# A decoder trunk on one core: the 72 weight pieces kept in DRAM are loaded, split and stored in three calls

## The chip, the cores and the metric

The kernel runs on one core of a Trainium2 chip. The metric is the device time of one execution in microseconds. Engines are named as the profile names them: PE (TensorE matmuls; PEld its weight loads), DVE (VectorE), ACT (ScalarE), POOL (GpSimd), and SP, whose queue issues every DMA of this kernel in order (SPq in the trace).

## The reference, cut to what matters

One sequence of 256 tokens, model width 1024, passes through two layers. Each has a half-step SwiGLU FFN (hidden width 2816) before and after its mixer; the mixer of layer 0 is a gated short convolution, that of layer 1 is RWKV-7 time mixing.

```python
def swiglu(x, w_gu, w_d):
    gate, up = jnp.split(x @ w_gu, 2, axis=-1)
    return (jax.nn.silu(gate) * up) @ w_d

for i in range(DEPTH):                       # DEPTH = 2
    x = x + 0.5 * swiglu(rms_norm(x, norm_g[i, 0]), ffn_w_gu[i, 0], ffn_w_d[i, 0])
    h = rms_norm(x, norm_g[i, 1])
    x = x + (short_conv_mixer(h, ...) if i % 2 == 0 else rwkv7_mixer(h, ...))
    x = x + 0.5 * swiglu(rms_norm(x, norm_g[i, 2]), ffn_w_gu[i, 1], ffn_w_d[i, 1])
return rms_norm(x, final_g)
```

Everything is float32. The kernel gets float32 accuracy from PE by splitting each operand in a rounded part `hi` and a rest `lo`, and adding three products: hi by hi, hi by lo, lo by hi.

## The kernel before, in words

The order of work is FFN 0, the convolution, FFN 1, FFN 2, the RWKV mixer, FFN 3. An FFN has 11 chunks (`c`) of 256 hidden columns, gate and up; each chunk takes two weight tiles (`kh` 0 and 1) of 1 MB. Then `project_out` (L246) takes the down projection in six groups, `[1, 2, 2, 2, 2, 2]` tiles of 1 MB. The convolution has six chunks and three groups, `[1, 1, 2]`.

Each weight tile goes through `weights` (L88): SP loads `raw`, ACT casts it into `hi` (L104), DVE subtracts to give `lo` (L105). There are three buffers each of `raw`, `hi` and `lo`, so SP runs at most three weight tiles ahead of DVE, and DVE at most three ahead of PE.

Between these loads the kernel prepares 72 pieces of weights for later: 48 of the RWKV matrices, 16 of its output matrix, 8 of FFN 3. A piece is 128 by 512 floats. `part_some(n)` (L602) first stores to DRAM whatever the call before has split (the tiles `hl`, hi and lo side by side, 512 KB), then takes n new pieces: it loads each into a tile `raw` (256 KB), casts it on ACT (L615) and subtracts on DVE (L616). It is called with n = 2 at the start of every chunk of FFN 0, the convolution, FFN 1 and FFN 2 until the pieces run out, which is in chunk 7 of FFN 2. `narrow` (L622) reads a piece back when the RWKV mixer wants it.

Two tags of buffers matter. `hl` has 7 buffers, for pieces on their way out, pieces read back, and two tiles `wboth`. `raw` has 2 buffers, for `raw_p` and for the two tiles `wa1` of `mixed_lora` (L628). `mixed_lora` is called between the convolution and FFN 1; it loads two small matrices into `wa1`, and POOL computes the two `wboth` from them (L642, L644), which stay until the mixer.

All loads and stores go through `load` (L48), which pins the DMA behind everything that was written before it for SP. So SP's order is the program's order, and a DMA whose wait isn't over holds up all that follow. ACT and DVE also work in the order of their instruction streams; that order is set when the program is built, by a planner that puts an instruction where its inputs are expected to be ready, except where it is pinned. The first weight tile of a layer (`kh` 0 of chunk 0) is loaded in the last group of the layer before; its `kh` 1 is loaded in chunk 0, and the norm's remaining steps (`late`) are run between its matmuls.

Of the kernel before, what the change touches and what calls it, by code (L numbers as in the profile page):

```python
# [21 lines left out]
FT = F // 128  # L22
# [3 lines left out]
class Trunk:  # L26


    def __init__(self, ctx, tc, bufs):
        self.tc, self.nc = tc, tc.nc  # L30
        nc = tc.nc
        self.const = ctx.enter_context(tc.tile_pool(name="const", bufs=1))
        self.rwp = ctx.enter_context(tc.tile_pool(name="rwp", bufs=1))
        self.front = ctx.enter_context(tc.tile_pool(name="front", bufs=1))
        self.dram = ctx.enter_context(tc.tile_pool(name="dram", bufs=1, space=bass.MemoryType.DRAM))
        self.parts, self.to_part, self.to_store = {}, deque(), deque()
        self.trp = ctx.enter_context(tc.tile_pool(name="trp", bufs=2, space=bass.MemoryType.PSUM))
        self.turn = False
        self.raw_bufs, self.hi_bufs, self.lo_bufs = bufs
        self.fixed = self.const.tile([128, 1298], F32, name="fixed")  # L40
        self.fixed_used = 0
        self.ident = self.fixed_cols(128)
        make_identity(nc, self.ident)
        self.x = self.const.tile([128, 2, D], F32, name="x")
        self.nhalf = self.fixed_cols(8)
        nc.gpsimd.memset(self.nhalf, -0.5)
# [164 lines left out]
    def norm_rows(self):  # L211


        nc = self.nc
        now, xn = {}, {}
        after = SimpleNamespace(first=None, late=deque())
        after.ready = [self.narrow(("k", 0, i), "k") for i in range(3)]

        def turn(t):

            out = []
            for h in range(2):
                out.append(self.tr_bank("hT"))
                for j in range(4):
                    nc.tensor.transpose(out=out[h][:, j * 128:(j + 1) * 128],
                                        in_=xn[t][:, h * 512 + j * 128:h * 512 + (j + 1) * 128], identity=self.ident)
            return out

        def step(t, h, c0=0, n=512):
            if h == 0:  # L230
                now["sq"] = self.halves(t)
            half, rstd = now["sq"]
            half(h)
            if h == 1:
                rs = rstd()
                xn[t] = self.wide([128, D], "xn")
                for i in range(2):
                    hs = slice(i * 512, i * 512 + 512)
                    nc.vector.tensor_scalar(xn[t][:, hs], self.x[:, t, hs], rs, None, op0=ALU.mult)
            if t == 1 and h == 0:  # L240
                after.banks = turn(0)

        after.turn = turn
        return step, after

    def project_out(self, ah, al, kt, w_out, alpha, groups, step, out, kc=2):  # L246

        nc = self.nc
        acc = [[self.mm_bank(f"acc{t}{h}") for h in range(2)] for t in range(2)]
        k0, posts = 0, deque()  # L250
        keep = lambda z: z
        for n in groups:
            ws = [self.weights(w_out[(k0 + kc * i) * 128:(k0 + kc * i + kc) * 128, :].rearrange("(k p) n -> p k n", p=128),
                               [128, kc, D], "o") for i in range(n)]
            last = k0 + kc * n == kt
            if last:
                keep = self.tc.keep_in_program_order
                if out is not None and out.first:
                    out.ready.append(out.first())
            for t in range(2):  # L260
                for h in range(2):

                    fine = out is None and t == h == 1
                    ts, size = slice(t * 128, t * 128 + 128), 256 if fine and last else 512
                    for c in range(0, 512, size):
                        hs = slice(h * 512 + c, h * 512 + c + size)
                        ps = (self.mm_bank(f"acc{c}") if fine and last else acc[t][h])[:, 0:size]
                        for k in range(k0, k0 + kc * n):
                            (wh, wl), j = ws[(k - k0) // kc], (k - k0) % kc
                            self.product(ps, ah[:, k, ts], al[:, k, ts], wh[:, j, hs], wl[:, j, hs],  # L270
                                         k == (k0 if fine and last else 0),
                                         k == kt - 1 or fine and k == kt - kc * groups[-1] - 1, keep)
                        if last or fine and k0 + kc * n == kt - kc * groups[-1]:
                            xs = self.x[:, t, hs]
                            nc.vector.scalar_tensor_tensor(xs, ps, alpha, xs, ALU.mult, ALU.add)
                        if last:
                            posts.append(step(t, h, c, size))
                    if last:
                        for _ in range(t + (t > h)):
                            post = posts.popleft()  # L280
                            if post:
                                post()
            k0 += kc * n
        if out is not None and posts[-1]:
            out.late.extend((lambda: None, posts.pop()))
# [35 lines left out]
                        normed.late.popleft()()  # L321
        return ps

    def ffn(self, normed, w_gu, w_d, follow, beside=True):
        nc, tc = self.nc, self.tc
        with tc.tile_pool(name="ffn", bufs=1, side="right", reuse_waits="tile") as pool, \
                (nullcontext() if normed.ps else self.banks(mm=6)):
# [3 lines left out]
            if normed.ps:  # L331
                normed.ready.extend(self.ffn_weights(w_gu, 1, kh) for kh in range(2))
            for c in range(FT // 2):
                if beside:
                    self.part_some(2)
                ps = (normed.ps if normed.ps and c == 0 else
                      self.inner(normed, "gu", lambda c, kh: self.ffn_weights(w_gu, c, kh), c))
                pt = self.tr_bank("aT").rearrange("p (j t) -> p j t", j=2)
# [9 lines left out]
                                            identity=self.ident)  # L348
                self.split(ah[:, 2 * c:2 * c + 2], al[:, 2 * c:2 * c + 2], pt)
            step, out = follow()  # L350
            self.project_out(ah, al, FT, w_d, 0.5, [1, 2, 2, 2, 2, 2], step, out)
        return out

    def conv(self, normed, w_in, cw, w_out, follow):

        nc, tc = self.nc, self.tc
        with tc.tile_pool(name="conv", bufs=1, reuse_waits="tile") as pool, self.banks(mm=6):
# [3 lines left out]
            cT = pool.tile([128, KT, T], F32, name="cT")  # L361
            project = lambda c: self.inner(normed, "ci", lambda c, kh: self.conv_weights(w_in, c, kh), c)
            for c in range(4):
                self.part_some(2)
                ps = project(c)
                pt = self.tr_bank("zT").rearrange("p (j t) -> p j t", j=2)
                for t in range(2):
# [12 lines left out]
                    nc.vector.scalar_tensor_tensor(cT[:, k, 2:], pt[:, j, :T - 2], cw[:, 0, k:k + 1], cT[:, k, 2:],  # L380
                                                   ALU.mult, ALU.add)
            for c in range(2):
                self.part_some(2)
                ps = project(4 + c)
                b = pool.tile([128, 2, 512], F32, name="b", tag="b", bufs=2)
                for t in range(2):
# [215 lines left out]
    def part_some(self, n):  # L602

        nc = self.nc
        while self.to_store:
            key, hl = self.to_store.popleft()
            self.parts[key] = self.dram.tile([128, 2, 512], F32, name="parts_%d" % len(self.parts))
            self.load(self.parts[key], hl)
        for _ in range(min(n, len(self.to_part))):
            key, src = self.to_part.popleft()  # L610
            raw = self.rwp.tile([128, 512], F32, tag="raw", name="raw_p", bufs=2)
            self.load(raw.rearrange("p (k n) -> p k n", k=2) if len(src.shape) == 3 else raw, src)
            hl = self.part_tile("hl_p")
            hi = hl[:, 0].bitcast(F32R)
            nc.scalar.copy(hi, raw)  # L615
            nc.vector.tensor_tensor(hl[:, 1].bitcast(F32R), raw, hi.bitcast(F32), ALU.subtract)  # L616
            self.to_store.append((key, hl))

    def part_tile(self, name):
        return self.rwp.tile([128, 2, 512], F32, tag="hl", name=name, bufs=7)  # L620

    def narrow(self, key, name):  # L622

# [4 lines left out]
    def mixed_lora(self, mu, w1, a1):  # L628
# [1 line left out]
        nc = self.nc  # L630
        out = []
        for k0 in range(0, KT, 4):
            w = self.rwp.tile([128, 4, 128], F32, tag="raw", name="wa1", bufs=2)
            for i, src in enumerate((w1, a1)):
                self.load(w[:, :, 64 * i:64 * i + 64],
                          src[k0 * 128:k0 * 128 + 512].rearrange("(k p) n -> p k n", p=128))
# [197 lines left out]
    def rwkv_heads(self, pool, prm, krv, lora, gT, g2, rows, row_tile, P, loaded, follow,  # L834
# [201 lines left out]
        def feed():  # L1036

            if done[0] >= len(P):
                for j, z in enumerate(first_weights):
                    sources.insert(2 * j, (None, *z))  # L1040
            while sources and (done[1] < 7 or sources[0][2]):
                i, key, to = sources.popleft()
                if to:
                    for j in range(2):
                        self.load(to[j], self.parts[key][:, j].rearrange("p (k n) -> p k n", k=2))
                else:
                    loaded.setdefault(i, []).append(self.narrow(key, "n"))
                    done[1] += 1
# [77 lines left out]
def trunk_kernel(ctx: ExitStack, tc: tile.TileContext, x, norm_g, final_g, ffn_w_gu, ffn_w_d, conv_w_in, conv_w,  # L1126
# [29 lines left out]
    with k.wide_weights():  # L1156
# [3 lines left out]
        posts = [step(t, h) for t, h in ((1, 0), (0, 1), (1, 1))]  # L1160
        n.late.extend((lambda: [post() for post in posts[0:2]], posts[2]))
        cv = []
        n = k.ffn(n, ffn_w_gu[0, 0], ffn_w_d[0, 0], lambda: before(
            lambda: cv.append(k.channel_vectors(72, [mu[0], conv_w[0]]).rearrange("p (m k) -> p m k", k=KT)),
            lambda: k.norm_T(g[:, 1], lambda: k.conv_weights(conv_w_in[0]))))
        cv, = cv
        n = k.conv(n, conv_w_in[0], cv[:, 6:9], conv_w_out[0], lambda: before(k.wkv_constants, lambda: k.norm_T(g[:, 2], fw(0, 1))))
        wa1 = k.mixed_lora(cv, w1[0], a1[0])
        n = k.ffn(n, ffn_w_gu[0, 1], ffn_w_d[0, 1], lambda: k.norm_T(g[:, 3], fw(1, 0)))
        n = k.ffn(n, ffn_w_gu[1, 0], ffn_w_d[1, 0], lambda: before(lambda: k.part_some(0), k.norm_rows))  # L1170
    n = k.rwkv(n, g[:, 4], cv[:, 0:6], wa1, dict(
        w_rkv=w_rkv[0], w0=w0, w2=w2[0], a0=a0, a2=a2[0], g1=g1[0], g2=g2[0],
        k_k=k_k[0], k_a=k_a[0], r_k=r_k[0].rearrange("h j -> (h j)"), ln_w=ln_w[0], ln_b=ln_b[0], w_o=w_o[0]),
# [26 lines left out]
```

## Time and profile before

| what | value |
|---|---|
| median of 3 runs | 1141.81 us (1140.89 to 1142.64) |
| the profiled execution, its own time | 1145.31 us |
| its span in the trace | 1143.6 us |
| mean granted clock of TensorE | 0.982 of full speed |
| PE busy | 1095.9 us, 96% of the span |
| DVE, ACT, POOL busy | 710.0, 562.0, 107.0 us |
| moved by DMA | 256.19 MB, mean 224 GB/s |

The profile comes from one execution, 3.5 us longer than the median. Busy time is the time in which an engine had an instruction running, for PE also when it ran at half clock. The granted clock has two levels, 1.0 (2.4 GHz) and 0.5 (1.2 GHz); a value between is a mean over a stretch.

### The profile page before, as it was taken

To read this page: it belongs to the slowest core of one execution; us is meant where nothing else is said; L and a number is where in the kernel's file an instruction comes from. 1 tells how busy PE (TensorE), PEld (TensorE's weight loads), DVE (VectorE), ACT (ScalarE), POOL (GpSimd) and SP (SyncE) were. 2 spreads that over 40 slices of the span, in tenths; PEclk is the share of its full clock that TensorE was granted. 3 is DMA by queue.
4 is the path that set the end of the run, shared out by engine and by line. 5 is a ranking of instruction groups with operands and counts; after the bars stand their busy time and mean duration, and the time that the engine had idled before them with its cause. 6 is when DMAs were issued, how large, how long until landed. Compare 5 with 4: busy or idle time off the path is not lost.

```text
span 1143.6 us, 15921 instructions
## 1 busy us (share of the span) xinstructions
PE 1095.9 (96%) x6064; PEld 906.1 (79%) x6064; DVE 710.0 (62%) x1021; ACT 562.0 (49%) x893; POOL 107.0 (9%) x201
## 2 busy tenths in 40 slices
PE   6999999899959999998999999999999999999997
PEld 4788888688848888886888888998887767888886
DVE  4666544677546665446665534757999986555535
ACT  6555433555435554345554433356666536444423
POOL 5000000000200000000000001022343221000000
PEclk9999999899979999998999999999999999999999
DMA  8999756697299995549997651963442656656541
GB/s 295 360 331 335 243 182 205 221 328 259 76 313 323 348 340 202 189 161 326 353 329 240 222 184 32 315 221 126 131 141 64 194 176 201 203 184 204 184 184 37
DMA packets 164340, 256.19 MB, mean 224 GB/s; under 512 B 10414, under 2 KB 128934, under 8 KB 164264
## 3 DMA queue, kind: packets, MB, share of 16 engines
q1 hardware_dynamic: 164264, 255.17, 66.5%
q8 instruction: 48, 0.79, 0.3%
q14 instruction: 28, 0.23, 0.1%
HBM read 216.34 MB, written 38.80 MB: 223 GB/s over the span
## 4 chain that ended last, share of the span: by engine, by line
PE 57%; issue 26%; DVE 10%; ACT 3%; DMA 2%; POOL 1%; SPq 0%; POOLq 0%; ACTq 0%; DVEq 0%
PE gu L111 10%; PE gu L112 10%; PE gu L110 10%; PE acc L112 5%; PE acc L110 5%; PE acc L111 5%; PE pj L110 2%; DVE pd L518 1%; PE aT L347 1%; PE pj L111 1%; PE pj L112 1%; PE xr L54 1%; DMA raw_p<-in_rwkv_w_rkv_dram 1%; PE ch L54 1%; PE G L54 1%
## 5 line engine op out<-in xcount | busy, mean ns | idle before, releaser
L110 PE MATMUL gu<-hi_gu,xh 128*128 128x512 f32 x688 | 271.8, 400 | 14.5 <-ACT hi_gu L104 13.8
L111 PE MATMUL gu<-lo_gu,xh 128*128 128x512 f32 x688 | 276.9, 403 | 5.0 <-DVE lo_gu L105 5.0
L105 DVE TENSOR_TENSOR lo_gu<-raw_gu,hi_gu 128x2048 fp32r<-128x2048 f32 (+2 forms) x92 | 197.9, 2154 | 130.9 <-ACT hi_gu L104 130.8
L112 PE MATMUL gu<-hi_gu,xl 128*128 128x512 f32 x688 | 274.9, 400 | 0.0
L104 ACT CAST hi_gu<-raw_gu 128x2048 fp32r<-128x2048 f32 (+2 forms) x92 | 165.0, 1797 | 72.8 <-PE gu L112 43.9
L105 DVE TENSOR_TENSOR lo_o<-raw_o,hi_o 128x2048 fp32r<-128x2048 f32 x48 | 109.3, 2291 | 116.5 <-ACT hi_o L104 116.5
L110 PEld LDWEIGHTS gu<-hi_gu,xh 128*128 128x128 f32 x688 | 131.4, 191 | 42.6 <-ACT hi_gu L104 15.2
L111 PEld LDWEIGHTS gu<-lo_gu,xh 128*128 128x128 f32 x688 | 132.2, 192 | 34.3 <-DVE lo_gu L105 8.2
L112 PEld LDWEIGHTS gu<-hi_gu,xl 128*128 128x128 f32 x688 | 132.1, 192 | 26.3 <-DVE xl L178 0.4
L104 ACT CAST hi_o<-raw_o 128x2048 fp32r<-128x2048 f32 x48 | 90.9, 1909 | 105.9 <-PE acc L112 102.3
L112 PE MATMUL acc<-hi_o,al 128*128 128x512 f32 (+1 forms) x356 | 138.1, 388 | 0.0
L111 PE MATMUL acc<-lo_o,ah 128*128 128x512 f32 (+1 forms) x356 | 138.0, 388 | 0.0
L110 PE MATMUL acc<-hi_o,ah 128*128 128x512 f32 (+1 forms) x356 | 132.2, 388 | 0.0
L148 POOL TENSOR_TENSOR rs<-ms,fixed 128x1 f32<-128x1 f32 x14 | 8.8, 632 | 862.4 <-DVE ms L146 862.3
L341 ACT ACTIVATE s<-gu,rs 128x256 f32<-128x256 f32 x88 | 41.7, 475 | 91.9 <-PE gu L112 91.3
L111 PEld LDWEIGHTS acc<-lo_o,ah 128*128 128x128 f32 x356 | 66.9, 188 | 13.5
L112 PEld LDWEIGHTS acc<-hi_o,al 128*128 128x128 f32 x356 | 66.9, 188 | 13.4
L110 PEld LDWEIGHTS acc<-hi_o,ah 128*128 128x128 f32 x356 | 66.9, 188 | 13.2
L115 ACT CAST ah<-aT 128x512 fp32r<-128x512 f32 x44 | 25.7, 583 | 87.6 <-PE aT L347 87.6
L345 DVE SCALAR_TENSOR_TENSOR a<-gu,rs,s 128x256 f32<-128x256 f32 x88 | 41.8, 480 | 28.5 <-ACT s L341 28.4
L616 DVE TENSOR_TENSOR hl_p<-raw_p,hl_p 128x512 fp32r<-128x512 f32 x72 | 47.3, 687 | 15.9 <-ACT hl_p L615 15.6
L116 DVE TENSOR_TENSOR al<-aT,ah 128x512 fp32r<-128x512 f32 x44 | 30.3, 689 | 40.7 <-ACT ah L115 40.7
(263 smaller groups left out, 1629.7 us busy)
## 6 DMA issues: line engine op xcount, KB each, us to landing
raw_gu<-in_ffn_w_gu_dram SPq DMA_DIRECT2D x164, 512.0 KB, 7.0
raw_o<-in_ffn_w_d_dram SPq DMA_DIRECT2D x44, 1024.0 KB, 5.0
parts<-hl_p SPq DMA_DIRECT2D x72, 512.0 KB, 4.8
hl_n<-parts SPq DMA_DIRECT2D x52, 512.0 KB, 4.0
raw_p<-in_rwkv_w_rkv_dram SPq DMA_DIRECT2D x48, 256.0 KB, 5.4
raw_ci<-in_conv_w_in_dram SPq DMA_DIRECT2D x14, 512.0 KB, 8.1
raw_ci<-in_conv_w_in_dram SPq DMA_DIRECT2D x4, 1024.0 KB, 8.2
raw_o<-in_conv_w_out_dram SPq DMA_DIRECT2D x4, 1024.0 KB, 4.8
```

What stands on the lines that cost most here:

```text
L54: self.tc.keep_in_program_order(self.nc.tensor.matmul(out, lhsT, rhs, start=True, stop=True))
L104: nc.scalar.copy(hi[:, ks], raw[:, ks])
L105: nc.vector.tensor_tensor(lo[:, ks], raw[:, ks], hi[:, ks].bitcast(F32), ALU.subtract)
L110: keep(mm(out, xh, wh, start=start, stop=False))
L111: keep(mm(out, xh, wl, start=False, stop=False))
L112: keep(mm(out, xl, wh, start=False, stop=stop))
L115: keep(self.nc.scalar.copy(hi, src))
L116: keep(self.nc.vector.tensor_tensor(lo, src, hi.bitcast(F32), ALU.subtract))
L341: act = nc.scalar.activation(s, ps[t][:, 0:256], AF.Silu, scale=rstd[t])
L345: nc.vector.scalar_tensor_tensor(a, ps[t][:, 256:512], rstd[t], s, ALU.mult, ALU.mult)
L347: nc.tensor.transpose(out=pt[:, j, t * 128:t * 128 + 128], in_=a[:, j * 128:(j + 1) * 128], identity=self.ident)
L616: nc.vector.tensor_tensor(hl[:, 1].bitcast(F32R), raw, hi.bitcast(F32), ALU.subtract)
```

## The change

`part_some` gets three stages in three successive calls: a call stores what the call before it split, splits what the call before it loaded, and loads n new pieces. The piece is loaded straight into the second half of its `hl` tile and split in place, so the `raw` tag goes away; `hl` gets 8 buffers, and `wa1` takes two of them. Calls are spread: 1 and 2 in turn in the chunks of an FFN (from chunk 2 on in FFN 0), and 1 at the start of each group of `project_out`, except in FFN 3. `norm_rows`, which runs between the chunks and the groups of FFN 2, calls `part_some(2)` until nothing is left to load or split. In the mixer's heads, `feed` may hold 8 read-back pieces in place of 7.

```diff
@@ norm_rows
+        while self.to_part or self.to_split:
+            self.part_some(2)
         now, xn = {}, {}
         after = SimpleNamespace(first=None, late=deque())
         after.ready = [self.narrow(("k", 0, i), "k") for i in range(3)]
@@ project_out(..., step, out, beside=True, kc=2)
         for n in groups:
+            if beside:
+                self.part_some(1)
             ws = [self.weights(...) for i in range(n)]
@@ ffn(self, normed, w_gu, w_d, follow, beside=True, first=0)
             for c in range(FT // 2):
-                if beside:
-                    self.part_some(2)
+                if beside and c >= first:
+                    self.part_some(1 + c % 2)
...
-            self.project_out(ah, al, FT, w_d, 0.5, [1, 2, 2, 2, 2, 2], step, out)
+            self.project_out(ah, al, FT, w_d, 0.5, [1, 2, 2, 2, 2, 2], step, out, beside)
@@ conv
             for c in range(4):
-                self.part_some(2)
+                self.part_some(1 + c % 2)
...
             for c in range(2):
-                self.part_some(2)
+                self.part_some(1)
@@ part_some
             key, hl = self.to_store.popleft()
             self.parts[key] = self.dram.tile([128, 2, 512], F32, name="parts_%d" % len(self.parts))
             self.load(self.parts[key], hl)
+        while self.to_split:
+            key, hl = self.to_split.popleft()
+            hi, lo = hl[:, 0].bitcast(F32R), hl[:, 1]
+            nc.scalar.copy(hi, lo)
+            nc.vector.tensor_tensor(lo.bitcast(F32R), lo, hi.bitcast(F32), ALU.subtract)
+            self.to_store.append((key, hl))
         for _ in range(min(n, len(self.to_part))):
             key, src = self.to_part.popleft()
-            raw = self.rwp.tile([128, 512], F32, tag="raw", name="raw_p", bufs=2)
+            hl = self.part_tile("hl_p")
+            raw = hl[:, 1]
             self.load(raw.rearrange("p (k n) -> p k n", k=2) if len(src.shape) == 3 else raw, src)
-            hl = self.part_tile("hl_p")
-            hi = hl[:, 0].bitcast(F32R)
-            nc.scalar.copy(hi, raw)
-            nc.vector.tensor_tensor(hl[:, 1].bitcast(F32R), raw, hi.bitcast(F32), ALU.subtract)
-            self.to_store.append((key, hl))
+            self.to_split.append((key, hl))
@@ part_tile
-        return self.rwp.tile([128, 2, 512], F32, tag="hl", name=name, bufs=7)
+        return self.rwp.tile([128, 2, 512], F32, tag="hl", name=name, bufs=8)
@@ mixed_lora
-            w = self.rwp.tile([128, 4, 128], F32, tag="raw", name="wa1", bufs=2)
+            w = self.part_tile("wa1")[:, 0].rearrange("p (k n) -> p k n", k=4)
@@ feed, in rwkv_heads
-            while sources and (done[1] < 7 or sources[0][2]):
+            while sources and (done[1] < 8 or sources[0][2]):
@@ trunk_kernel
-        n = k.ffn(n, ffn_w_gu[0, 0], ffn_w_d[0, 0], lambda: before(
+        n = k.ffn(n, ffn_w_gu[0, 0], ffn_w_d[0, 0], first=2, follow=lambda: before(
...
-        n = k.ffn(n, ffn_w_gu[1, 0], ffn_w_d[1, 0], lambda: before(lambda: k.part_some(0), k.norm_rows))
+        n = k.ffn(n, ffn_w_gu[1, 0], ffn_w_d[1, 0], k.norm_rows)
```

## Rows read from the trace of the kernel before

**Rows 1.** PE by stretch: start:end us, length, PE busy (instructions), granted clock, DMA share, GB/s.

```profile
60.00:80.00 20.00, 20.00 (x93) 1.00 1.01 337
218.00:222.00 4.00, 0.55 (x4) 1.00 1.09 369
222.00:229.00 7.00, 4.93 (x11) 0.53 1.06 374
...
314.00:322.00 8.00, 0.46 (x3) 0.75 0.50 157
322.00:328.00 6.00, 4.46 (x9) 0.50 1.03 371
332.00:336.00 4.00, 0.84 (x3) 0.88 1.05 393
336.00:341.00 5.00, 5.00 (x12) 0.50 1.09 345
...
524.00:530.00 6.00, 2.32 (x10) 0.97 1.08 373
530.00:537.00 7.00, 5.69 (x15) 0.54 1.07 369
...
26.00:30.20 4.20, 1.91 (x9) 1.00 1.05 396
```

**Rows 2.** The same view of a stretch of `project_out` in FFN 1.

```profile
452.00:512.00 60.00, 60.00 (x272) 1.00 0.54 184
```

**Rows 3.** Waits of SP's queue, whole span: us in total, times, longest.

```profile
SPq L50 <- DVE hl_p L616: 152.3, 61, 15.5
...
SPq L50 <- POOL wboth L644: 27.0, 2, 26.4
```

**Rows 4.** Timeline of SP, FFN 0 to convolution: start, us, instruction.

```profile
191.53 3.41 SPq L50 DMA_DIRECT2D raw_ci<-in_conv_w_in_dram  x4
209.96 0.94 SPq L50 DMA_DIRECT2D parts<-hl_p  x2
...
212.93 2.69 SPq L50 DMA_DIRECT2D raw_ci<-in_conv_w_in_dram  x4
```

**Rows 5.** Timeline of DVE, same stretch.

```profile
209.24 1.29 DVE L616 TENSOR_TENSOR hl_p<-raw_p,hl_p 128x512 fp32r<-128x512 f32 x2
```

**Rows 6.** Timeline of SP, convolution to FFN 1.

```profile
287.14 1.60 SPq L50 DMA_DIRECT2D parts<-hl_p  x2
...
317.76 2.00 SPq L50 DMA_DIRECT2D raw_gu<-in_ffn_w_gu_dram  x4
```

**Rows 7.** Timeline of all engines, start of FFN 0.

```profile
12.12 0.63 ACT L138 ACTIVATE junk<-x 128x512 f32<-128x512 f32 x1 [1.31 <-DMA x<-in_x_dram]
...
14.13 2.17 ACT L176 ACTIVATE xh<-xT,fixed 128x128 fp32r<-128x128 f32 x8
...
17.21 2.56 SPq L50 DMA_DIRECT2D raw_gu<-in_ffn_w_gu_dram  x4
```

**Rows 8.** Timeline of SP, end of the chunks of FFN 2.

```profile
618.72 2.37 SPq L50 DMA_DIRECT2D hl_k<-parts  x4
...
623.32 56.27 SPq L50 DMA_DIRECT2D raw_o<-in_ffn_w_d_dram  x11
```

**Rows 9.** Timeline of PE, first matmul of `project_out` in FFN 2.

```profile
647.06 0.39 PE L110 MATMUL acc<-hi_o,ah 128*128 128x512 f32 x1
```

**Rows 10.** Page, part 5: casts and subtractions of `project_out`'s weights: busy, mean ns | idle before.

```profile
L105 DVE TENSOR_TENSOR lo_o<-raw_o,hi_o 128x2048 fp32r<-128x2048 f32 x48 | 109.3, 2291 | 116.5 <-ACT hi_o L104 116.5
...
L104 ACT CAST hi_o<-raw_o 128x2048 fp32r<-128x2048 f32 x48 | 90.9, 1909 | 105.9 <-PE acc L112 102.3
```

**Rows 11.** Page, part 6: DMA issues, KB each, median us to landing.

```profile
raw_o<-in_ffn_w_d_dram SPq DMA_DIRECT2D x44, 1024.0 KB, 5.0
parts<-hl_p SPq DMA_DIRECT2D x72, 512.0 KB, 4.8
...
raw_p<-in_rwkv_w_rkv_dram SPq DMA_DIRECT2D x48, 256.0 KB, 5.4
```

More of the change, by code (lines that the diff above doesn't have):

```diff
@@ L35, in __init__ @@
         self.dram = ctx.enter_context(tc.tile_pool(name="dram", bufs=1, space=bass.MemoryType.DRAM))
-        self.parts, self.to_part, self.to_store = {}, deque(), deque()
+        self.parts, self.to_part, self.to_split, self.to_store = {}, deque(), deque(), deque()
         self.trp = ctx.enter_context(tc.tile_pool(name="trp", bufs=2, space=bass.MemoryType.PSUM))
@@ L244, in norm_rows, with project_out @@
         return step, after
-    def project_out(self, ah, al, kt, w_out, alpha, groups, step, out, kc=2):
+    def project_out(self, ah, al, kt, w_out, alpha, groups, step, out, beside=True, kc=2):
         nc = self.nc
@@ L322, in inner, with ffn @@
         return ps
-    def ffn(self, normed, w_gu, w_d, follow, beside=True):
+    def ffn(self, normed, w_gu, w_d, follow, beside=True, first=0):
         nc, tc = self.nc, self.tc
```

## The prediction

> **What bounds the kernel now.** I read the page's slices first, then PE's windows, then the waits of SP's queue, then the timelines of the places that these point to. In the middle of FFN 0 PE is busy for the whole of a stretch at full clock while the DMA engines are full as well [rows 1]; in the groups of `project_out` PE is full and DMA half used [rows 2]. There an engine that isn't PE can only matter through a stall of PE. So I looked for stretches in which PE is idle or at half clock. Outside the mixer there are four, all at the start of a layer, three of them shortly after a stretch without loads.
>
> - First chunk of the convolution, 218 to 229: idle 3.45 and 2.07 us, and 4.93 us of work at a mean clock of 0.53, which loses 4.93 x 0.47 = 2.3. Together 7.8 us [rows 1].
> - First chunk of FFN 1: idle 7.54, 1.54 and 3.16 us; 4.46 and 5.00 us at half clock lose 2.2 and 2.5. Together 17.0 us [rows 1].
> - First chunk of FFN 2: idle 3.68 and 1.31 us; 5.69 x 0.46 = 2.6. Together 7.6 us [rows 1].
> - Start of FFN 0: 2.3 us idle from 26 to 30.2 [rows 1], and more before it while the input arrives.
>
> The reader is to see what SP did before each. At the convolution it issues `kh` 1 of chunk 0 until 194.94, and then nothing for 15.0 us: the next instruction is the store of two pieces, at 209.96 [rows 4]. DVE splits those two at 209.24 [rows 5], after the norm's steps, so the store waits for the split and the weights of chunk 1, at 212.93, wait behind the store [rows 4]. When PE has used up chunk 0 at 218, they aren't there. FFN 2 repeats this; the longest such wait is 15.5 us [rows 3]. At FFN 1 it is worse: after its store at 287.14 SP stands 26.4 us for POOL's `wboth` [rows 3], because the next piece wants a `raw` buffer and both hold `wa1`; even `kh` 1 of chunk 0 goes out only at 317.76 [rows 6], when PE is already idle.
>
> **The change, part by part.**
>
> *The wait for POOL.* The piece no longer uses `raw`. At the first call of FFN 1 the `hl` tag holds one piece being stored, one to split, two `wa1`, two `wboth` and the new one: 7 of 8. At the second call two more come and the stored one is gone: 8 of 8. So SP shouldn't stand there. Then `kh` 1 goes out at about 291 in place of 317.76, 23 us before PE's idle time at 314; landing and the two conversions take 9.2 us for a tile of 1 MB [rows 10, 11]. Gain: 17.0 us, as far as no new stall comes.
>
> *The stores.* A call now stores what was split one call earlier. The pieces to be split in chunk 0 were loaded in the last group of the layer before, some 10 us and three loads earlier than now, so their split can take one of the idle places that ACT and DVE have ahead of the norm's steps. Then chunk 1's weights go out at about 197 in place of 212.93, so 16 us earlier, and the stall at 218 to 229 was 5.5 us of waiting. Gain: 7.8 and 7.6 us. Between nothing and the mean wait for a split, 152.3 / 61 = 2.5 us [rows 3], may stay at each of the three places; I take 0.5 each, because the splits are ready long before: -1.5 us.
>
> *The first two chunks of FFN 0 without pieces.* ACT starts on the second half of `xh` at 14.13, when its last step before the pieces' casts ended at 12.75: 1.4 us at least [rows 7]. The weights of chunk 1 go out at 17.21 [rows 7] behind two stores, and four loads and two stores less are ahead of them; if that also takes the idle 2.3 us [rows 1] and a half-clock stretch like that of FFN 2 (2.6), the gain is 6.3. I take 4, the middle.
>
> *The pieces moved into `project_out`.* Six pieces of 256 KB in and 512 KB out are 4.7 MB on a stretch of 60 us: 184 + 79 = 263 GB/s, under the 337 of the chunks [rows 1, 2]. A split is about 0.65 us on DVE [rows 5], and I count as much for ACT's cast; a group of two tiles costs DVE 4.6 and ACT 3.8 us [rows 10] of 11 us. PE's full stretch hides them. If that cover were gone, each piece would cost its 1.3 us. The split in place has the same operands: nothing. The eighth buffer in `feed`: I found no wait of PE for a piece read back, and seven are ahead already: nothing.
>
> *The emptying in `norm_rows`.* The calls take 19 pieces in FFN 0, 11 in the convolution, 22 in FFN 1 and 16 in the chunks of FFN 2; 4 are left. Three calls then put 4 loads and 5 stores on SP ahead of three read-backs (`hl_k`), and 2 more stores ahead of the first `raw_o`. Behind them on SP stands everything that PE wants for `project_out`. Now SP is done with the chunks' loads at 618.72 and issues `raw_o` from 623.32 [rows 8]. PE wants it at 647.06 [rows 9]; landing 5.0 [rows 11], cast 1.9 and subtraction 2.3 [rows 10] make 637.9 the latest issue, 19.1 us after 618.72. The new chain is 14 issues of some 0.5 us [rows 4, 8], one load landing 5.4, one split on two engines 1.3, one store landing 4.8 before a third read-back finds a buffer [rows 11]: 18.5 us, no stall. With a mean wait for a split of 2.5 us it is 2 us late, with the longest of 15.5 [rows 3] 15 us. I take 2, since the row's mean is the ordinary case.
>
> By the Trainium skill, DMA: Bandwidth & Descriptors, section "Anatomy of one DMA", a DMA takes 2.0 us plus its bytes over 436 GB/s (fitted for GpSimd's path, not SP's); that gives an estimate of 2.6 us for this load and 3.2 for this store, 4.4 less, so that no stall would be left and the total would be 1107. The rows say 5.4 and 4.8 [rows 11] for the same transfers under this kernel's load, and I go by them.
>
> *Sum.* 17.0 + 7.8 + 7.6 - 1.5 + 4 - 2 = 32.9 us. From the profiled execution's 1145.3 that leaves 1112.4; the median of the runs is 3.5 us under that execution, so 1109.
>
> **The rivals.**
>
> A, the forecast: 1109. Its own ends: with nothing left of the stalls and 6.3 at the start, 38.7 us, 1103; with 2.5 left at each place, 1.4 at the start and a late `raw_o` of 5 us, 21.3 us, 1120. Chance 0.73.
>
> B: the store still waits. ACT and DVE keep their order; if the planner puts chunk 0's split behind the norm's steps, the split runs at 209 as now [rows 5] and SP waits as now, one store in place of two. Then the convolution and FFN 2 keep their stalls, and FFN 1 keeps one like theirs: gain 17.0 - 7.8 + 4 - 2 = 11.2, 1131. Against it: its data is there a group earlier. Chance 0.09. The Trainium skill, Perfetto Trace Analysis, section "Tensor Engine Instruction", calls ACT and DVE strict first in, first out; by that rule a split that was put late stays late, and the trace agrees (rows 5: 209.24, for a piece that SP had asked for before 191.53).
>
> C: the wait for POOL moves to `hl`. If a piece of FFN 1 is given a `wa1` buffer, or a store is late so that the eighth buffer isn't free, SP waits for POOL as now: 32.9 - 17.0 = 15.9, 1126. For it: the count comes to 8 of 8. Against it: that is at the second call, behind `kh` 1. Chance 0.10.
>
> D, slower: a store stands ahead of each group's `raw_o`, in 15 groups of FFN 0, the convolution and FFN 1. `raw_o` may be 14.6 us late (637.9 - 623.32) before PE stalls. With the longest wait of 15.5 us at each, PE would lose 0.9 and a half-clock stretch of 2.6, 52 us in all: 1161. It decides from 2.2 us a group on. Against it: the mean wait is 2.5, and these splits have had a whole group's time. Chance 0.05.
>
> E, no change: the stalls last until the DMA engines deliver, not until SP issues; their share is 1.05 to 1.09 inside the stalls [rows 1]. Then they stay, and what the start gives goes into `norm_rows`: about 1140. Against it: the engines are at 0.50 in 314 to 322 [rows 1], because nothing had been issued. Chance 0.03.
>
> **The numbers.** A difference of 0.2% (2.3 us) is about what a measurement of this kernel can tell from no change. A, B and C are faster, 0.92; E is the same, 0.03; D is slower, 0.05. The range of 8 in 10 is 1102 to 1127: A, and C with it; B, D and E stay out, 0.17.
>
> **What would show it.** Right: SP issues `kh` 1 of FFN 1's chunk 0 within some 5 us of the convolution's last loads and waits for POOL no more; chunk 1's weights go out some 15 us earlier at the convolution and at FFN 2; PE's windows there are full and at clock 1.0; SP's waits for a split fall well under 152.3 us. Wrong: stores still issued only after the norm (B), an `hl` tile waiting for POOL (C), idle PE at the start of FFN 2's `project_out` of more than 5 us, or PE no longer full in the groups of FFN 0 and FFN 1 (D). An order of ACT or DVE that the planner changes elsewhere, in the mixer above all, would make the prediction wrong in a way that no row here shows.

## The result

The median fell from 1142.22 us (1140.89 to 1143.53) to 1109.82 us (1109.41 to 1110.38): ratio 0.9717, 95% interval 0.97 to 0.9734. The forecast was 1109.0, range 1102 to 1127. The two profiled executions lie 35.5 us apart (spans 1143.6 and 1108.1), because that of before was 3.1 us longer than its median and that of after was not (1109.84).

The kernel's stages, each measured from PE's first matmul in it to its first matmul in the next, show where the time came from.

| stage | before | after | difference | forecast |
|---|---|---|---|---|
| FFN 0, chunks | 139.1 | 131.3 | -7.8 | -4 |
| convolution, chunks | 77.3 | 70.4 | -6.9 | -7.3 |
| FFN 1, chunks | 143.7 | 126.9 | -16.8 | -16.5 |
| FFN 2, chunks | 133.5 | 127.0 | -6.5 | -7.1 |
| FFN 2, groups | 58.0 | 60.7 | +2.7 | +2 |
| mixer | 241.9 | 241.6 | -0.3 | 0 |

The groups of the first three layers (61.7, 24.3, 61.6) and FFN 3 (190.5, to the end of PE's last matmul) are as before. The differences add up to -35.6, the spans to -35.5.

First, PE by stretch in the profile after, with the columns of [rows 1] and those of PEld, DVE, ACT and POOL between: the first chunks of the convolution, of FFN 1 and of FFN 2, the start, and a stretch of `project_out` in FFN 1.

```profile
207.00:211.00 4.00, 4.00 (x21) 3.25 (x19) 1.27 (x3) 2.49 (x3) 0.00 (x0) 1.00 0.63 219
211.00:218.00 7.00, 5.66 (x26) 4.40 (x25) 6.97 (x5) 4.37 (x4) 0.00 (x0) 1.00 0.58 179
300.00:306.00 6.00, 6.00 (x28) 4.67 (x26) 3.24 (x7) 3.05 (x5) 5.92 (x9) 1.00 0.07 23
306.00:314.00 8.00, 6.64 (x31) 5.43 (x31) 6.48 (x5) 4.64 (x4) 2.52 (x1) 1.00 0.99 323
490.00:495.00 5.00, 4.48 (x21) 3.36 (x19) 2.27 (x3) 3.38 (x4) 0.00 (x0) 1.00 0.55 180
495.00:502.00 7.00, 6.18 (x28) 5.09 (x29) 6.72 (x6) 4.08 (x4) 0.00 (x0) 1.00 0.70 208
12.00:16.20 4.20, 2.74 (x13) 1.69 (x12) 3.46 (x10) 4.20 (x12) 3.73 (x10) 1.00 1.07 354
430.00:490.00 60.00, 60.00 (x274) 49.73 (x273) 32.26 (x41) 26.70 (x39) 1.52 (x2) 1.00 0.70 236
```

The granted clock is 1.00 in every line: the half-clock stretches of [rows 1] followed the idle spells and went with them. One idle spell of about 1.34 us is left in each of the three layers; the two stretches of FFN 2 share theirs. In `project_out` PE is as full as in [rows 2], with 52 GB/s more moved beside it (236 against 184; forecast 79 more).

Next, the waits of SP's queue after, as in [rows 3].

```profile
SPq L50 <- DVE hl_p L617: 35.2, 8, 10.0
...
SPq L50 <- POOL wboth L651: 6.8, 1, 6.8
```

The wait for a split fell from 152.3 us in 61 waits to 35.2 in 8, and the wait for POOL from 27.0 to 6.8. Neither is gone. Where they stand now is seen in SP's timeline, first from FFN 0 to the convolution (against [rows 4]), then from the convolution to FFN 1 (against [rows 6]).

```profile
184.37 0.55 SPq L50 DMA_DIRECT2D parts<-hl_p  x1
185.34 1.63 SPq L50 DMA_DIRECT2D hl_p<-in_rwkv_w_rkv_dram  x2
187.38 4.89 SPq L50 DMA_DIRECT2D raw_ci<-in_conv_w_in_dram  x4
202.32 0.34 SPq L50 DMA_DIRECT2D parts<-hl_p  x1
...
274.46 2.00 SPq L50 DMA_DIRECT2D raw_gu<-in_ffn_w_gu_dram  x4
276.51 0.47 SPq L50 DMA_DIRECT2D parts<-hl_p  x1
277.04 1.62 SPq L50 DMA_DIRECT2D hl_p<-in_rwkv_w_rkv_dram  x2
280.32 6.64 SPq L50 DMA_DIRECT2D raw_gu<-in_ffn_w_gu_dram  x4
297.00 0.34 SPq L50 DMA_DIRECT2D parts<-hl_p  x1
304.25 0.37 SPq L50 DMA_DIRECT2D hl_p<-in_rwkv_w_rkv_dram  x1
```

At the convolution, chunk 1's weights go out at 187.38, 6.1 us after `kh` 1 of chunk 0 (181.31); before, 21.4 us lay between the two (191.53 and 212.93). At FFN 2 the same distance fell from 21.5 us (498.23 and 519.77) to 5.8 (464.43 and 470.18). The store that holds SP until 202.32 is now that of chunk 2's call and stands behind them. At FFN 1, `kh` 1 of chunk 0 goes out at 274.46, chunk 1's weights at 280.32. SP still stands for POOL's `wboth`, between 297.34 and 304.25, in chunk 2's call.

DVE's timeline says why the store of chunk 1's call, at 184.37, found its piece ready, and why the next did not.

```profile
169.48 0.68 DVE L617 TENSOR_TENSOR hl_p<-hl_p 128x512 fp32r<-128x512 f32 x1
...
201.52 0.15 DVE L146 SCALAR_TENSOR_TENSOR ms<-ss,ms 128x1 f32<-128x1 f32 x1
201.60 0.69 DVE L617 TENSOR_TENSOR hl_p<-hl_p 128x512 fp32r<-128x512 f32 x1
```

The piece of chunk 0's call was split at 169.48, in the last groups of FFN 0. The piece of chunk 1's call is still split behind the norm's steps, as in [rows 5].

### The profile page after: what moved, and what is told of

Read it like the earlier page. It is cut to its first block, busy times and chain, and to the rows that moved or that the text cites. A ratio compares the mean times of both kernels' runs of the same rounds, so it can differ in the third digit from the quotient of the medians.

```text
span 1108.1 us, 15866 instructions
## 1 busy us (share of the span) xinstructions
PE 1081.7 (98%) x6064; PEld 897.4 (81%) x6064; DVE 711.0 (64%) x1021; ACT 562.8 (51%) x893; POOL 113.0 (10%) x201
## 4 chain that ended last, share of the span: by engine, by line
PE 70%; issue 18%; DVE 8%; ACT 2%; DMA 0%; SPq 0%; POOL 0%; POOLq 0%; ACTq 0%; DVEq 0%
PE gu L111 11%; PE gu L112 11%; PE gu L110 11%; PE acc L112 6%; PE acc L111 6%; PE acc L110 6%; PE ci L111 2%; PE ci L112 2%; PE ci L110 2%; PE pj L110 2%; PE xr L54 2%; PE pj L112 1%; PE pj L111 1%; PE aT L351 1%; PE ch L54 1%
## 5 line engine op out<-in xcount | busy, mean ns | idle before, releaser
L111 PE MATMUL gu<-lo_gu,xh 128*128 128x512 f32 x688 | 272.2, 396 | 2.8 <-DVE lo_gu L105 2.7
L112 PE MATMUL gu<-hi_gu,xl 128*128 128x512 f32 x688 | 271.9, 395 | 0.0
L110 PE MATMUL gu<-hi_gu,xh 128*128 128x512 f32 x688 | 268.9, 393 | 0.7 <-ACT xh L176 0.7
L111 PEld LDWEIGHTS gu<-lo_gu,xh 128*128 128x128 f32 x688 | 129.6, 188 | 30.3 <-DVE lo_gu L105 4.8
L112 PEld LDWEIGHTS gu<-hi_gu,xl 128*128 128x128 f32 x688 | 129.6, 188 | 25.0 <-DVE xl L178 0.4
L110 PE MATMUL acc<-hi_o,ah 128*128 128x512 f32 (+1 forms) x356 | 131.1, 388 | 0.0
L616 ACT CAST hl_p<-hl_p 128x512 fp32r<-128x512 f32 x72 | 44.3, 624 | 29.5 <-DMA hl_p<-in_rwkv_w_rkv_dram 19.7
```

The source lines that it names most:

```text
L110: keep(mm(out, xh, wh, start=start, stop=False))
L111: keep(mm(out, xh, wl, start=False, stop=False))
L112: keep(mm(out, xl, wh, start=False, stop=stop))
L616: nc.scalar.copy(hi, lo)
```

## The experiments

Eight kernels, each computing the whole reference, compared with the kernel before (medians 1143.59 us beside the first four, 1142.86 beside the last four). The chunks of each layer, as in the first table, with the groups of FFN 2:

| kernel | median | FFN 0 | conv. | FFN 1 | FFN 2 | FFN 2 groups |
|---|---|---|---|---|---|---|
| `wa1` out of `raw` (lora_own) | 1132.82 | 137.6 | 76.3 | 133.3 | 133.4 | 58.0 |
| old spread (old_spread) | 1120.95 | 132.0 | 70.5 | 139.2 | 126.9 | 58.0 |
| two stages (two_stage) | 1131.95 | 131.2 | 75.3 | 133.1 | 136.9 | 60.6 |
| pieces from chunk 0 (first0) | 1109.00 | 132.5 | 70.4 | 126.9 | 126.9 | 58.0 |
| seven buffers (hl7) | 1118.20 | 131.1 | 70.4 | 137.3 | 127.0 | 59.1 |
| one piece in FFN 1 (spread_f1) | 1110.50 | 133.8 | 70.5 | 127.5 | 126.9 | 58.0 |
| pinned order (pin) | 1106.04 | 133.1 | 68.8 | 126.0 | 125.3 | 60.8 |
| and no tail (pin_no_tail) | 1104.66 | 130.6 | 68.8 | 126.2 | 127.1 | 58.0 |

**Is the wait for POOL a thing apart from the waits for stores?** The kernel before, with `wa1` moved to `hl` and nothing else.

```diff
-            w = self.rwp.tile([128, 4, 128], F32, tag="raw", name="wa1", bufs=2)
+            w = self.part_tile("wa1")[:, 0].rearrange("p (k n) -> p k n", k=4)
```

> The kernel before with one edit: the two tiles wa1 take buffers of hl (7, as before), so no piece waits for POOL to give back raw. If the stall at the start of FFN 1 is two things, the wait for POOL ahead of kh 1 of chunk 0 and behind it the wait of a store for a late split, then only the first goes: the chunks of FFN 1 take as long as those of FFN 2 (133.5 us in place of 143.8), the whole about 1132 us, and SP's waits for the split stay near 152 us. If the wait for POOL alone makes the 17 us, 1125. If the loads are late for want of transfer rate, 1142.

Measured 1132.82 us (1131.86 to 1137.23), ratio 0.9917 (0.9894 to 0.9939). The timeline of SP at FFN 1 in this kernel:

```profile
287.91 2.07 SPq L50 DMA_DIRECT2D raw_gu<-in_ffn_w_gu_dram  x4
309.43 0.94 SPq L50 DMA_DIRECT2D parts<-hl_p  x2
```

The wait for POOL is gone, `kh` 1 goes out at 287.91, and 19.4 us pass behind it until the next store. FFN 1's chunks take 133.3 us, as those of FFN 2 do in this kernel (133.4). SP's waits for a split did not stay near 152 us: they are 176.1 us in 65 waits, and the longest is this one, 19.4. So the 16.8 us at FFN 1 are 10.4 of POOL (143.7 - 133.3) and 6.4 of the late store (133.3 - 126.9).

**Stages or spread?** The changed kernel with the calls spread as before: two pieces in every chunk, none in the groups.

```diff
-                if beside and c >= first:
-                    self.part_some(1 + c % 2)
+                if beside:
+                    self.part_some(2)
...
-            if beside:
-                self.part_some(1)
```

> The kernel after with the pieces spread as before: two at the start of every chunk from chunk 0 of FFN 0 on, none in the groups of project_out; the three stages, the 8 buffers and wa1 in hl stay. If the stages carry the gain, the three stalls stay away: two to three us more than after at the start of FFN 0, about 2.8 less at the end of FFN 2, where nothing is left to empty, so 1109 to 1112. If the spread carries it (two pieces a chunk fill the DMA engines), the stalls of the convolution and of FFN 1 and 2 come back, 7 to 8 us each: 1125 to 1133.

Measured 1120.95 us (1120.51 to 1121.69), ratio 0.9806 (0.9791 to 0.9821): neither. Start, convolution and FFN 2 keep their gain; only FFN 1 loses 12.3 us (139.2 against 126.9). Its waits of SP's queue, and SP's timeline at FFN 1:

```profile
SPq L50 <- POOL wboth L649: 22.8, 2, 21.1
```

```profile
279.82 1.96 SPq L50 DMA_DIRECT2D raw_gu<-in_ffn_w_gu_dram  x4
281.82 0.95 SPq L50 DMA_DIRECT2D parts<-hl_p  x2
303.97 2.59 SPq L50 DMA_DIRECT2D hl_p<-in_rwkv_w_rkv_dram  x2
306.65 2.07 SPq L50 DMA_DIRECT2D raw_gu<-in_ffn_w_gu_dram  x4
```

This is rival C's mechanism: the third piece loaded in FFN 1 waits for POOL (303.97), it is chunk 1's, and chunk 1's weights (306.65) wait behind it.

**The stages alone undone.** The changed kernel, with the piece split in the call that loads it and stored in the next.

```diff
-            self.to_split.append((key, hl))
+            hi, lo = hl[:, 0].bitcast(F32R), hl[:, 1]
+            nc.scalar.copy(hi, lo)
+            nc.vector.tensor_tensor(lo.bitcast(F32R), lo, hi.bitcast(F32), ALU.subtract)
+            self.to_store.append((key, hl))
```

> The kernel after with the split back in the call that loads the piece; spread, 8 buffers, in-place split and wa1 in hl stay. If the distance between load and split carries the gain at the convolution, FFN 1 and FFN 2, a store in chunk 1 waits again until the norm's steps are through, and each of the three places loses 7 to 8 us: about 1131. If the spread and the buffers carry it, 1110.

Measured 1131.95 us (1130.71 to 1132.32), ratio 0.9903 (0.9886 to 0.9919). The timeline of SP at the convolution in this kernel:

```profile
180.95 3.43 SPq L50 DMA_DIRECT2D raw_ci<-in_conv_w_in_dram  x4
201.95 0.34 SPq L50 DMA_DIRECT2D parts<-hl_p  x1
202.34 1.31 SPq L50 DMA_DIRECT2D hl_p<-in_rwkv_w_rkv_dram  x2
203.69 2.36 SPq L50 DMA_DIRECT2D raw_ci<-in_conv_w_in_dram  x4
```

The picture of [rows 4] is back: 17.6 us between `kh` 1's end (184.38) and the store, chunk 1's weights behind it. The time is the one expected, but its parts are not 7 to 8 us each: the convolution, FFN 1 and FFN 2 lose 4.9, 6.2 and 9.9 us. Of FFN 2's 9.9, 2.8 us are idle time of PE directly ahead of its groups (0.87 and 1.92); what made them was not traced.

**The first two chunks of FFN 0.** The changed kernel with pieces from chunk 0 on.

```diff
-        n = k.ffn(n, ffn_w_gu[0, 0], ffn_w_d[0, 0], first=2, follow=lambda: before(
+        n = k.ffn(n, ffn_w_gu[0, 0], ffn_w_d[0, 0], first=0, follow=lambda: before(
```

> The kernel after with pieces from chunk 0 of FFN 0 on (first=0), else the same; one piece in place of four is left for norm_rows. The start gained 7.8 us, 4 were forecast. If leaving the pieces out of chunks 0 and 1 gives it, the start loses 5 to 8 us: 1114 to 1117. If the start's loss was the casts of the pieces in the same call and the stores behind them, which three stages move away too, it loses 1 to 3 us, and the end of FFN 2 gives 1 to 2 back: 1109 to 1112.

Measured 1109.0 us (1108.43 to 1110.63), ratio 0.9703 (0.9689 to 0.9718). The start keeps its gain within 1.2 us, and FFN 2's groups take 58.0 us again, since only one piece in place of four is left to empty: the emptying costs 2.7 us.

**The number of buffers.** The changed kernel with seven.

```diff
-        return self.rwp.tile([128, 2, 512], F32, tag="hl", name=name, bufs=8)
+        return self.rwp.tile([128, 2, 512], F32, tag="hl", name=name, bufs=7)
...
-            while sources and (done[1] < 8 or sources[0][2]):
+            while sources and (done[1] < 7 or sources[0][2]):
```

> The changed kernel with 7 buffers of hl in place of 8, and 7 pieces read back in feed. Theory: at FFN 1 the buffers, and not the stages, keep SP from standing for POOL. In the changed kernel SP loads three pieces there (one in chunk 0, two in chunk 1) and waits 6.8 us for POOL at the fourth, in chunk 2's call, where nothing is late. With one buffer less the third piece would wait, in chunk 1's call, ahead of chunk 1's weights: a wait for POOL of some 20 us, the chunks of FFN 1 11 to 14 us longer (126.9 to 138 to 141), 1121 to 1124 in all; the other stages as they are. Rival: the eighth buffer is spare; SP waits a few us more in places where nothing is late, and the time stays at 1110.

Measured 1118.2 us (1117.46 to 1119.93), ratio 0.9782 (0.9759 to 0.9804). SP at FFN 1:

```profile
276.70 26.62 SPq L50 DMA_DIRECT2D hl_p<-in_rwkv_w_rkv_dram  x2
303.42 2.13 SPq L50 DMA_DIRECT2D raw_gu<-in_ffn_w_gu_dram  x4
```

The second load of chunk 1's call, the third piece of FFN 1, waits, as expected. FFN 1's chunks take 137.3 us, 10.4 more (11 to 14 expected), and FFN 2's groups gave back 1.6, which was not expected; so the whole came under the 1121 to 1124 of the expectation.

**What the spread does beyond that.** The old spread, but one piece in each of chunks 0 to 2 of FFN 1 (shown against the kernel of the old spread). The last pieces then fall in chunk 9 of FFN 2, so `norm_rows` here also stores what is split.

```diff
-        while self.to_part or self.to_split:
+        while self.to_part or self.to_split or self.to_store:
...
-                    self.part_some(2)
+                    self.part_some(1 if c < few else 2)
...
-        n = k.ffn(n, ffn_w_gu[0, 1], ffn_w_d[0, 1], lambda: k.norm_T(g[:, 3], fw(1, 0)))
+        n = k.ffn(n, ffn_w_gu[0, 1], ffn_w_d[0, 1], lambda: k.norm_T(g[:, 3], fw(1, 0)), few=3)
```

> The changed kernel with the old spread (two pieces in every chunk, none in the groups), but one piece in chunks 0 to 2 of FFN 1. Theory: all that the new spread does for the time is that the piece that waits for POOL comes later than chunk 1's weights. With one piece in each of chunks 0 and 1 the third piece is chunk 2's, so the wait for POOL is harmless and the 12 us that the old spread cost come back: chunks of FFN 1 about 127, 1108 to 1110. Rival: the spread also works through the convolution (fewer pieces per call ahead of FFN 1, or pieces moved into the groups): then FFN 1 stays above 133 and the time above 1115.

Measured 1110.5 us (1109.73 to 1111.11), ratio 0.9712 (0.9691 to 0.9733); FFN 1's chunks 127.5. The load that waits is chunk 2's again (306.05), behind chunk 1's weights (283.83). So nothing of the gain needs pieces in the groups of `project_out`.

**The 1.34 us that are left.** ACT's timeline of the changed kernel, where PE waits in the convolution (PE's wait is the last line):

```profile
208.05 0.47 ACT L373 ACTIVATE s<-ci,rs 128x256 f32<-128x256 f32 x1 [2.52 <-PE ci L112]
208.43 1.90 ACT L104 CAST hi_ci<-raw_ci 128x2048 fp32r<-128x2048 f32 x1
```

```profile
212.70 0.50 PE L111 MATMUL ci<-lo_ci,xh 128*128 128x512 f32 x1 [1.34 <-DVE lo_ci L105]
```

The cast of chunk 1's first tile, issued by SP at 187.38, stands behind `s`, for which ACT idles 2.52 us. The next kernel writes that tile ahead of `s` and pins `s` (the FFNs get the like; their first `s` was pinned already).

```diff
                 ps = project(c)
+                if c == 0:
+                    normed.ready.append(self.conv_weights(w_in, 1, 0))
...
-                    nc.scalar.activation(s, ps[t][:, 0:256], AF.Copy, scale=rstd[t])
+                    act = nc.scalar.activation(s, ps[t][:, 0:256], AF.Copy, scale=rstd[t])
+                    if c == 0:
+                        self.tc.keep_in_program_order(act)
```

> The changed kernel with kh 0 of chunk 1 of each layer asked for right behind chunk 0's matmuls in the program, ahead of s, which is pinned there, so that ACT casts that tile before it waits for PE. Theory: the 1.34, 1.37 and 1.34 us that PE still idles at chunk 1 of the convolution, FFN 1 and FFN 2 come from ACT's order: the cast stands behind s, which waits for PE's last matmul of chunk 0, while its data has landed. Then the three idle times go: about 4 us less, 1106. Rival: the cast only comes as early as DVE's or the DMA's next step allows: 1110, the idle times stay or move.

Measured 1106.04 us (1104.98 to 1107.89), ratio 0.9673 (0.9652 to 0.9695), 3.8 us under the changed kernel (1109.82, from another set of runs). The cast now runs first, and PE by stretch, in the same columns as above, is full in all three places. In FFN 1 a wait of 0.47 us for DVE's `lo_gu` comes up one chunk later (317.59).

```profile
205.95 1.95 ACT L104 CAST hi_ci<-raw_ci 128x2048 fp32r<-128x2048 f32 x1
209.65 0.47 ACT L377 ACTIVATE s<-ci,rs 128x256 f32<-128x256 f32 x1 [1.75 <-PE ci L112]
```

```profile
205.00:215.00 10.00, 10.00 (x45) 8.26 (x45) 7.35 (x12) 7.04 (x12) 0.00 (x0) 1.00 0.88 273
300.00:310.00 10.00, 10.00 (x46) 8.29 (x45) 8.17 (x9) 5.36 (x7) 8.14 (x9) 1.00 0.30 92
485.00:500.00 15.00, 15.00 (x70) 12.35 (x69) 11.10 (x14) 8.99 (x14) 0.00 (x0) 1.00 0.91 301
```

**Both.** The same, and two pieces in every chunk of FFN 2, so that nothing is left to empty.

```diff
-                    self.part_some(1 + c % 2)
+                    self.part_some(max(n, 1 + c % 2))
...
-        n = k.ffn(n, ffn_w_gu[1, 0], ffn_w_d[1, 0], k.norm_rows)
+        n = k.ffn(n, ffn_w_gu[1, 0], ffn_w_d[1, 0], k.norm_rows, n=2)
```

> The same order of ACT, and two pieces in every chunk of FFN 2, so that nothing is left for norm_rows to empty. Theory: the two gains add: 4 us from the order and 2.7 from FFN 2's groups (60.7 back to 58.0): 1103. Rival: two pieces in chunks 0 and 1 of FFN 2 bring a stall back there, or the order gives nothing: 1107 to 1110.

Measured 1104.66 us (1104.33 to 1105.38), ratio 0.9662 (0.9641 to 0.9683): the fastest of all. The groups give 2.8 us, but the chunks of FFN 2 take back 1.8: one chunk later than the pin reaches, PE waits 1.50 us for DVE, with the cast behind `s` on ACT again.

```profile
499.47 0.47 ACT L347 ACTIVATE s<-gu,rs 128x256 f32<-128x256 f32 x1 [1.86 <-PE gu L112]
499.84 1.90 ACT L104 CAST hi_gu<-raw_gu 128x2048 fp32r<-128x2048 f32 x1
```

## Why the prediction was right

**The wait for POOL** (17.0 forecast with 0.5 left, 16.8 came). Right in size. But the 17.0 were put down to this wait alone, and it is worth 10.4 by itself (the first experiment); the other 6.4 are a late store like those of the convolution and FFN 2, which rival B had at 7.8. In how it goes, rival C was half right: a piece does wait for a buffer that POOL still reads, but the fourth of FFN 1, in chunk 2's call, 6.8 us long, with chunk 1's weights ahead of it.

The prediction's count of 8 is not what failed. At 297.34 seven of the eight tiles were in use: the piece just being stored, two to split, two `wa1` and two `wboth`. The eighth was free, for the store issued at 276.51 had landed 7.2 us later. The load went out all the same only at 304.25, right behind the end of POOL's first subtraction from `wa1`:

```profile
302.93 1.30 POOL L651 TENSOR_TENSOR wboth<-wa,wboth 128x512 f32<-128x512 f32 x1
```

So the piece had been given a `wa1` buffer, the first condition of rival C, while another buffer was free. In the old spread it was the same: the two stores from 281.82 on landed some 6.3 us after their issue, and the third piece waited until 303.97. In what order the buffers are handed out, no run shows.

With one buffer less the third piece waits and 10.4 us are lost; with two pieces a call the third again, at 12.3. So the eighth buffer and the thinner calls of FFN 1's first chunks are both needed here, with no piece to spare, and the forecast held by that margin.

**The stores** (7.3 and 7.1 forecast, 6.9 and 6.5 came). The mechanism is as forecast: the split of chunk 0's call ran 14.9 us ahead of its store, in the groups before the norm (169.48 and 184.37). What rival B feared happened to the next split, at 201.60, and cost nothing, because the third stage puts the store that waits for it one call later. The two-stage run, with the same spread, loses 4.9 of the 6.9 and more than the 6.5 again, so the gains hang on the stages. The Trainium skill, Perfetto Trace Analysis, section "Tensor Engine Instruction", calls ACT and DVE strict first in, first out, by which a late place stays late; the split at 201.60 agrees, and so does the cast at 208.43.

**What may stay at each place** (0.5 forecast; 1.34, 1.36 and 1.34 came). The size was short by 2.5 us in all, though within the bounds (0 to 2.5). The three layers' sums came out well all the same, because each gave back 0.2 to 1.2 us more than the idle and half-clock time that [rows 1] had for it; why was not traced. The wait is also another than the one named, a cast behind `s` on ACT and not a store behind a split; the pinned order shows it, with 1.6, 0.9 and 1.7 us less in the three layers.

**The start of FFN 0** (4 forecast, 1.4 to 6.3; 7.8 came in these two profiles). Mis-sized. Eight profiles with the new start have 130.6 to 133.8 us, mean 132.0; the two with the old one 139.1 and 137.6: some 6.4 us. The gain was put down to the edit that leaves out the pieces of chunks 0 and 1, and the runs don't give it to that alone: with pieces from chunk 0 on and three stages it is there as well (132.5, and 132.0 with the old spread), and with two stages and no early pieces too (131.2). What all of these share is that chunk 1's weights go out from 8.9 to 12.6 us on, ahead of the first store, where they stood behind two stores until 17.21 [rows 7].

The parts of the forecast can be told apart by PE's waits. The first is the one for the norm's second half, where `xh` on ACT stands ahead of `xl` on DVE; in the profile of before it is

```profile
16.48 0.66 PE L57 MATMUL xT<-fixed,x 128*128 128x128 f32 x4 [3.98 <-DVE xl L178]
```

and 2.49 us in the first experiment's kernel, which has the old start too. In the eight it is 0.72 to 2.68, mean 1.73, so some 1.5 us less (1.4 forecast). The two waits for chunk 1's first tile, 0.75 and 1.59 us before, are 0.30 us at most in the eight, and nothing in six of them (2.3 forecast). Work at half clock in the first 40 us (busy time by what its mean clock lacks to 1.00) cost 2.6 and 2.7 us with the old start, and with the new one nothing in six profiles and 1.2 in two: some 2.4 us less (2.6 forecast). So all three terms came, about at the upper end of 6.3, and taking the middle was the step that was too small. The start differs by 3.2 us among the eight; the two longest, 133.8 and 133.1, are the two with a mean clock of 0.91 in the first 20 us. Why the clock fell in these two stays open.

**The emptying** (2 forecast, 0 to 15; 2.7 came). Right in size, wrong in place. The first `raw_o` goes out 12.7 us ahead of the first matmul that wants it (596.41 and 609.14), still ahead of the 9.2 that landing and conversions need; PE then loses 0.82 and 1.38 us, and the first of these is again a cast behind `s`:

```profile
606.48 0.47 ACT L345 ACTIVATE s<-gu,rs 128x256 f32<-128x256 f32 x1 [2.60 <-PE gu L112]
606.85 1.90 ACT L104 CAST hi_o<-raw_o 128x2048 fp32r<-128x2048 f32 x1
...
611.13 0.50 PE L111 MATMUL acc<-lo_o,ah 128*128 128x512 f32 x1 [0.82 <-DVE lo_o L105]
```

What the remaining 0.5 us is was not traced. For the landing the prediction went by [rows 11] (store 4.8, load 5.4 us). The page of the profile after, part 6, has longer ones still, 7.1 and 7.4. By the Trainium skill, DMA: Bandwidth & Descriptors, section "Anatomy of one DMA", the estimates were 3.2 and 2.6 us (for GpSimd's path); these traces don't agree.

```profile
parts<-hl_p SPq DMA_DIRECT2D x72, 512.0 KB, 7.1
...
hl_p<-in_rwkv_w_rkv_dram SPq DMA_DIRECT2D x48, 256.0 KB, 7.4
```

**The pieces in the groups, and rivals D and E.** Nothing, as forecast: PE's stretch is full, the groups of the first three layers last what they lasted. E falls with FFN 1: the stalls went when SP issued earlier.

**The total** (1109.0 forecast, 1109.82 came). That it came so close is partly luck. Between the two profiles the stages gave 35.6 us where the sum had 32.9. But the profile of before was 3.1 us longer than its median, which the profile of after was not, and the forecast had taken the same excess off both. Most of the 3.1 us lie early: the first experiment's kernel does the same work as before up to FFN 1, and its FFN 0 and convolution chunks took 1.5 and 1.0 us less.

## What to carry to other kernels

On a queue that issues in program order, as SP's does here, a store is as late as the slowest thing it waits for, and everything behind it is as late as the store. Give such a store one call more than its producer needs, so that what is late waits behind the loads that matter and not ahead of them. Where a slow engine still reads some buffers of a shared tag, counting the free ones is not enough: look in the trace which buffer the next tile has been given, and put the piece that must wait behind the next weights. Then look on the converting engines for the same picture: a cast whose data is there, behind an instruction that waits for PE.

## What the runs showed that was not expected

An idle PE cost more here than its idle time. The three layer starts of before had 22.8 us idle and another 9.6 lost at half clock [rows 1]; idle spells of 1.34 to 1.36 us in the kernel after left the clock at 1.00 in each stretch shown. In the old-spread run the clock was 0.50 in the stretch in which an idle spell of 4.45 us ends, shortly after one of 4.67, in the columns used above:

```profile
300.00:312.00 12.00, 6.76 (x29) 4.98 (x27) 3.63 (x8) 2.02 (x5) 6.07 (x9) 0.90 0.44 138
312.00:320.00 8.00, 3.02 (x6) 1.99 (x7) 3.94 (x3) 4.21 (x4) 0.00 (x0) 0.50 1.03 364
```

The length of the spell alone does not tell: at the start of FFN 0 a wait of 1.89 us (pinned order) came with a mean clock of 0.91 in the first 20 us, one of 2.68 us (pieces from chunk 0) with 1.00.

The median store of a piece landed 7.1 us after its issue in place of 4.8, though the bytes are the same; why was not tried.
